# First four feed-forward products as one group in steps of two k-tiles, and most of x turned by VectorE blocks and DRAM instead of TensorE

## The chip, the cores and the metric

The kernel runs on one NeuronCore of a Trainium2 chip. The metric is the device time of one execution in microseconds (us); of several runs the median is taken. The program is launched once; all inputs and the output lie in the chip's DRAM.

## What is computed

One decoder layer on 256 tokens of width 2048, in float32: a half-weighted SwiGLU feed-forward, a mixer (dilated attention beside a gated spatial branch), a second feed-forward and a final norm. The change touches only the first feed-forward's start and the loading of three small parameter rows:

```python
def rmsnorm(x, g):
    r = x32 * lax.rsqrt(jnp.mean(x32 * x32, axis=-1, keepdims=True) + NORM_EPS)
    return (r * g.astype(jnp.float32)).astype(x.dtype)

def swiglu(x, w_gate, w_up, w_down):
    return (jax.nn.silu(x @ w_gate) * (x @ w_up)) @ w_down

# in reference():
x = x + 0.5 * swiglu(rmsnorm(x, ffn1_norm[i]), ffn1_w_gate[i], ffn1_w_up[i], ffn1_w_down[i])
```

`w_gate` and `w_up` are 2048 x 5632, `w_down` is 5632 x 2048.

## The kernel before, in words

**Products.** Every large product is cut into output pieces of 512 columns (`gemm`), each with two PSUM banks, one for each 128 tokens. The sum over the inner dimension goes in k-tiles of 128 rows. A **step** (an entry of `hus`, counted by `i`) is two k-tiles of one piece. Weights come from DRAM in units of four k-tiles (`load_unit`, 1 MB, a `raw` tile, of which there are three); `split` makes of a step's weights a high part (`wh`, ScalarE, L139) and a rest (`wl`, VectorE, L140), of which four pairs exist; the activations are held as such pairs too (`xhi`, `xlo`). `product` (L149) issues one matmul; a step has 12: two k-tiles, two token halves, and the three combinations wh by xhi ("hh"), wl by xhi ("hl") and wh by xlo ("lh"). `high_first` puts the two hl last in each k-tile.

**Order of the work.** The order on each engine is that in which the Python code issues it. The main loop goes over the steps: it issues the products of step `i`, then the callbacks that `at(i, ...)` has left there, then (`advance`) the weight loads that have a free tile and the splits of a later step. `lay_out` writes the list of steps: it goes through the pieces one after the other, the four units of each in turn, and only where `pair` is set are two pieces taken together, with both their last units at the end.

**The transposed x.** A matmul wants the activations with the inner dimension on the partitions. At the start this is done by TensorE: `first_transposes` (L235) turns two 128 x 128 blocks of x for a k-tile, with the identity, into a PSUM bank; `first_evac` multiplies by the norm's weight (`gcols`) and writes `xhi` (ScalarE, L239) and `xlo` (VectorE, L240). All 16 k-tiles of the first norm go this way, 32 transposes, in eight groups of four, placed by `begin` and `ready` between the first steps' matmuls. Everywhere else the kernel uses `turn`: VectorE transposes 32 x 32 blocks (L191), SP writes the result to DRAM (L175), reads it back with the blocks in their places (four reads, L181), and ScalarE and VectorE make the pair of it (L264, L163, L164). The rms itself is applied later, when a product is evacuated, so its squares may be summed after the products have begun.

**The start.** SP issues all loads of weights and x. Seven matmuls on a zeroed tile (`junk`, L81, L748) come ahead of everything on TensorE, then the transpose of the first norm weights (L752), one more such matmul, and then the first transposes of x. x is loaded in parts: columns 0 to 255, 256 to 511, and three times 512. The remaining norm weights are loaded at step 20 and transposed by TensorE at step 60 (`gains`, L761).

Of the kernel before, what the change touches and what calls it, by code (L numbers as in the profile page):

```python
# [8 lines left out]
F32 = mybir.dt.float32  # L9
# [7 lines left out]
P = 128  # L17
# [18 lines left out]
LA = 3  # L36
# [5 lines left out]
def layer(ctx: ExitStack, tc: tile.TileContext, a, out):  # L42
# [25 lines left out]
    rows = sb.tile([60, P], F32, name="rows")  # L68
# [6 lines left out]
    load_rows(0, ACT)  # L75
    half = sb.tile([P, 2], F32, name="half")
# [3 lines left out]
    junk = sb.tile([P, NC], BF16, name="junk")  # L80
    DVE.memset(junk, 0.0)  # L81
# [12 lines left out]
    gcols = sb.tile([P, 60], F32, name="gcols")  # L94
# [6 lines left out]
    def gemm(w, c0, rows0, nk, lhs, post, pair=False):  # L101
        gemms.append(dict(w=w, c0=c0, rows0=rows0, nk=nk, lhs=lhs, post=post, pair=pair))
# [17 lines left out]

    def load_unit(i, parts=(0, 4)):
        g, u, _ = hus[2 * i]
        if i in raws:
            r = raws[i]
        else:
            r = raws[i] = big.tile([P, UK, NC], F32, tag="raw", bufs=RAWB, name=f"raw{i}")
        k0 = g["rows0"] + u * UK * P
        src = g["w"][k0:k0 + UK * P, g["c0"]:g["c0"] + NC].rearrange("(k p) c -> p k c", p=P)
        k = slice(*parts)
        SP.dma_start(r[:, k], src[:, k])  # L130
# [12 lines left out]
    def product(i, jj, t, kind):  # L143
        g, u, j = hus[i]
        if "ps" not in g:
            g["ps"] = [mm_bank(f"mm{i}_{q}") for q in range(NT)]
# [21 lines left out]
    def turn(i, name, q, put, dst, ev, lag=8):  # L168
# [15 lines left out]
        at(i + 3, back)  # L184
# [47 lines left out]
    def first_transposes(k):  # L232
        b = first_banks[k] = first_banks.get(k) or tp_bank(f"xt{k}")
        for t in range(NT):
            PE.transpose(b[:, t * P:(t + 1) * P], x[:, t, k * P:(k + 1) * P], ident)  # L235
# [6 lines left out]
    def residual(e, n, c, banks, scale, norm):  # L242
# [16 lines left out]

        def evac(src):  # L260
            for j in range(4):
# [6 lines left out]
        turn(e + (6 if c == 1 else 2), f"x{n}_{c}", 8, put_tokens(lambda: x[:, :, cs]),  # L268
             lambda: flat(sb.tile([P, NT, NC], F32, tag="gate", bufs=2, name=f"xt{n}_{c}")), evac, 6)


    def ffn(wg, wu, wd, down_post, pair):
        halves = ((0, 6), (6, 11))
        for hf, (f0, f1) in enumerate(halves):
# [8 lines left out]
            for f in range(f0, f1):  # L283
# [30 lines left out]
                gemm(wg, f * NC, 0, KD, lhs_x, post_gate, pair and f == 0)  # L314
                gemm(wu, f * NC, 0, KD, lhs_x, post_up)
            for c in range(4):
                gemm(wd, c * NC, f0 * NC, 4 * (f1 - f0), lhs_h,
                     lambda e, banks, c=c, hf=hf: down_post(e, c, banks, hf == 1), c == 0)
# [5 lines left out]
    ffn(a["ffn1_w_gate"][0], a["ffn1_w_up"][0], a["ffn1_w_down"][0], down1, False)  # L324
# [325 lines left out]
    for j in range(3):  # L650
        gemm(w_in, o_s + j * NC, 0, KD, lhs_x, post_gelu("vs", j), j == 0)
# [12 lines left out]
    for c in range(4):  # L664
        gemm(a["w_out"][0], c * NC, 0, KD, lambda: (mix["mhi"], mix["mlo"]),
             lambda e, banks, c=c: residual(e, 2, c, banks, 1.0, True), c == 0)
# [52 lines left out]
    ffn(a["ffn2_w_gate"][0], a["ffn2_w_up"][0], a["ffn2_w_down"][0], down2, True)  # L719
# [36 lines left out]
    first_banks[1] = mm_bank("xt1")  # L756
    first_banks[2] = mm_bank("xt2")

    def gains():
        b = tp_bank("gc1")  # L760
        PE.transpose(b[:, 0:60], rows, ident[0:60, 0:60])  # L761
        DVE.tensor_copy(gcols[:, 16:60], b[:, 16:60])

    at(20, lambda: [load_rows(i) for i in range(1, 4)])
    at(60, gains)
# [4 lines left out]
    loaded, done = 4, 8  # L770
# [11 lines left out]
    def ready(i, whole=False):  # L782
        ks = (2 * i, 2 * i + 1)
        for k in ks:
            first_transposes(k)
        for j, k in enumerate(ks):
            first_evac(k)
            if not whole:
                split(i, slice(j, j + 1))
        if whole:  # L790
            split(i)

    def begin():
        split(0, slice(0, 1))
        for k in (0, 1):
            first_transposes(k)
            first_evac(k)
        split(0, slice(1, 2))
        products(0, jjs=(0,))
        for t in range(NT):  # L800
            product(0, 1, t, "hh")
        for k in (2, 3):
            first_transposes(k)
            first_evac(k)
        for kind in ("lh", "hl"):
            for t in range(NT):
                product(0, 1, t, kind)
        for k in (0, 1):
            split(1, slice(k, k + 1))

    begin()
    early = {2: (3, False), 3: (4, True), 5: (7, True)}
    midway = {1: (2, False), 3: (5, True), 4: (6, True)}
    for i in range(n):
        if i in early:
            ready(*early[i])
        if 0 < i < n - LA - 1:
# [64 lines left out]
```

## Time and profile before

| | us |
|---|---|
| median of 3 runs (2048.91 to 2049.04) | 2049.03 |
| the profiled execution, its own time | 2049.03 |
| its span (first to last recorded instruction) | 2047.3 |
| TensorE busy in the span | 2037.1 |
| VectorE busy | 1181.6 |
| ScalarE busy | 973.9 |

The span is what the trace covers; 1.7 us of the execution's own time lie around it. PE is TensorE, DVE VectorE, ACT ScalarE, POOL GpSimd; SPq is the queue on which SP issues DMAs. Busy time counts instructions from start to end, and matmuls overlap one another, so a matmul's shown duration is not what it adds to the time; the distance between the starts of two neighbours is.

### The profile page before, as it was taken

What the parts mean: (1) busy time and instruction counts of PE and PEld (TensorE: products, weight loads), DVE (VectorE), ACT (ScalarE), POOL (GpSimd) and SP (SyncE); (2) the same over time, 40 slices, a digit from 0 to 9 for tenths busy, and PEclk for the clock granted to TensorE, in tenths of its full rate; (3) what the DMA queues carried; (4) which work ended last, traced back from release to release, by engine and by line L of the source; (5) the groups of instructions that cost most, each with busy time, mean ns of one, the idle gap of its engine ahead of it and who ended that gap; (6) DMA issues with size and microseconds to landing.
All of it is one profiled execution on the core that took longest, in us unless ns stands there. A gap on an engine that the chain in (4) does not pass through costs nothing.

```text
span 2047.3 us, 23805 instructions
## 1 busy us (share of the span) xinstructions
PE 2037.1 (100%) x9486; PEld 1781.6 (87%) x9486; DVE 1181.6 (58%) x1192; ACT 973.9 (48%) x1070; POOL 12.4 (1%) x18
## 2 busy tenths in 40 slices
PE   9999999999999999999999999999999999999998
PEld 7888888888888888888888888888888888888887
DVE  5555555555556557665665555565555555555554
ACT  6444444444445555455554444564444444444443
POOL 0000000000000000000000000000000000000000
PEclk9999999999999999999999999999999999999999
DMA  7777876666776866787866666777777666777764
GB/s 271 234 236 226 272 245 216 201 222 224 243 229 220 269 201 201 238 280 257 262 212 224 225 225 207 245 250 235 220 243 226 226 205 205 221 222 242 232 214 144
DMA packets 246775, 469.35 MB, mean 229 GB/s; under 512 B 11084, under 2 KB 38536, under 8 KB 246536
## 3 DMA queue, kind: packets, MB, share of 16 engines
q1 hardware_dynamic: 246344, 467.30, 70.4%
q8 instruction: 74, 1.21, 0.2%
q10 hardware_dynamic: 320, 0.53, 0.1%
q14 instruction: 37, 0.30, 0.0%
HBM read 439.22 MB, written 28.57 MB: 228 GB/s over the span
## 4 chain that ended last, share of the span: by engine, by line
PE 99%; issue 0%; ACT 0%; DVE 0%; POOLq 0%; POOL 0%
PE mm L149 98%; PE sc L560 0%; PE sp L458 0%; PE warm L748 0%; PE pv L600 0%; PE sc L562 0%; PE xt L235 0%; PE pv L596 0%; ACT x L716 0%; ACT xhi L239 0%; PE pv L597 0%; DVE x L701 0%; POOLq L877 0%; POOL rf L708 0%; ACT wh L139 0%
## 5 line engine op out<-in xcount | busy, mean ns | idle before, releaser
L140 DVE TENSOR_TENSOR wl<-raw,wh 128x1024 fp32r<-128x1024 f32 (+1 forms) x780 | 948.1, 1218 | 822.1 <-ACT wh L139 818.0
L139 ACT ACTIVATE wh<-raw 128x1024 fp32r<-128x1024 f32 (+1 forms) x780 | 818.0, 1052 | 1007.6 <-PE mm L149 974.6
L149 PE MATMUL mm<-wh,xhi 128*128 128x512 f32 x2144 | 813.8, 380 | 0.5 <-ACT wh L139 0.4
L149 PE MATMUL mm<-wh,xlo 128*128 128x512 f32 x2144 | 812.5, 379 | 0.0
L149 PE MATMUL mm<-wl,xhi 128*128 128x512 f32 x2144 | 811.8, 379 | 0.0
L149 PEld LDWEIGHTS mm<-wh,xhi 128*128 128x128 f32 x2144 | 405.3, 189 | 58.5 <-ACT wh L139 0.8
L149 PEld LDWEIGHTS mm<-wl,xhi 128*128 128x128 f32 x2144 | 405.4, 189 | 57.2
L149 PEld LDWEIGHTS mm<-wh,xlo 128*128 128x128 f32 x2144 | 405.1, 189 | 57.3
L149 PE MATMUL mm<-wh,hhi 128*128 128x512 f32 x704 | 266.8, 379 | 0.0
L149 PE MATMUL mm<-wl,hhi 128*128 128x512 f32 x704 | 266.8, 379 | 0.0
L149 PE MATMUL mm<-wh,hlo 128*128 128x512 f32 x704 | 266.8, 379 | 0.0
L149 PEld LDWEIGHTS mm<-wh,hhi 128*128 128x128 f32 x704 | 133.1, 189 | 18.9
L149 PEld LDWEIGHTS mm<-wl,hhi 128*128 128x128 f32 x704 | 133.1, 189 | 18.9
L149 PEld LDWEIGHTS mm<-wh,hlo 128*128 128x128 f32 x704 | 133.1, 189 | 18.9
L149 PE MATMUL mm<-wh,uT 128*128 128x512 f32 x192 | 58.0, 379 | 0.0
L149 PE MATMUL mm<-wh,mhi 128*128 128x512 f32 x128 | 48.5, 379 | 0.0
L149 PE MATMUL mm<-wl,mhi 128*128 128x512 f32 x128 | 48.5, 379 | 0.0
L149 PE MATMUL mm<-wh,mlo 128*128 128x512 f32 x128 | 48.5, 379 | 0.0
L149 PEld LDWEIGHTS mm<-wh,uT 128*128 128x128 f32 x192 | 36.3, 189 | 5.1
L149 PE MATMUL mm<-wl,uT 128*128 128x512 f32 x96 | 36.4, 379 | 0.0
L304 DVE SCALAR_TENSOR_TENSOR sg<-mm,rstd,sg 128x512 f32<-128x512 f32 x44 | 30.9, 744 | 0.0
L219 ACT ACTIVATE junk<-x 128x512 bf16<-128x512 f32 x30 | 18.9, 629 | 25.0 <-DVE x L247 18.6
(142 smaller groups left out, 596.9 us busy)
## 6 DMA issues: line engine op xcount, KB each, us to landing
raw<-in_w_in_dram SPq DMA_DIRECT2D x92, 1024.0 KB, 5.1
raw<-in_ffn_w_up_dram SPq DMA_DIRECT2D x88, 1024.0 KB, 5.2
raw<-in_ffn_w_down_dram SPq DMA_DIRECT2D x88, 1024.0 KB, 5.1
raw<-in_ffn_w_gate_dram SPq DMA_DIRECT2D x84, 1024.0 KB, 5.1
raw<-in_w_out_dram SPq DMA_DIRECT2D x16, 1024.0 KB, 5.0
raw<-in_w_sg_out_dram SPq DMA_DIRECT2D x12, 1024.0 KB, 5.8
bmh<-bth SPq DMA_DIRECT2D x22, 512.0 KB, 2.9
sg<-bmh SPq DMA_DIRECT2D x88, 128.0 KB, 5.0
```

Of the source, the lines that this page charges most:

```text
L139: ACT.activation(wh[:, k], r[:, k], AF.Copy)
L140: DVE.tensor_tensor(wl[:, k], r[:, k], wh[:, k].bitcast(F32), op=OP.subtract)
L149: PE.matmul(g["ps"][t], act[:, k, t * P:(t + 1) * P], in_turn(w[:, jj]), start=k == 0 and kind == "hh", stop=k == g["nk"] - 1 and kind == ...
L219: ACT.activation(junk, x[:, t, c * NC:(c + 1) * NC], AF.Square, accum_out=ss[n][:, t, c:c + 1])
L304: DVE.scalar_tensor_tensor(two(sg[:, t]), banks[t], rstd[:, t:t + 1], two(sg[:, t]), op0=OP.mult, op1=OP.mult)
```

## The change

1. `lay_out` sorts steps, not units. The first four pieces of the first feed-forward (gate 0, up 0, gate 1, up 1) form one group (`FIRST`): first k-tiles 0 and 1 of all four (steps 0 to 3), then k-tiles 2 and 3 of all four (steps 4 to 7), then k-tiles 4 to 7 of each piece (steps 8 to 15), then k-tiles 8 to 15 of each (steps 16 to 31). The other groups (`PAIR`) give the same order as before. The third and fourth piece accumulate in the banks that the transposes use (tag `tp`).
2. `load_unit` can fill a `raw` tile from two weights; the first four units are loaded so.
3. Only k-tiles 0 to 3 of the first x are transposed by TensorE. Columns 512 to 2047 go through `turn_x`, as the later norms do: columns 512 to 1023 at step 0 (read back at 1, made into pairs at 4), the next 512 at steps 7, 10 and 12, the last at 8, 11 and 13. The loads of the last 1024 columns of x are issued after steps 3 and 4.
4. The remaining norm weights are loaded at step 32 and go through a VectorE block transpose, a DRAM write and four small reads; TensorE's `gains` is gone.
5. `junk` is zeroed before `half` and `pad`.

```diff
-    def gemm(w, c0, rows0, nk, lhs, post, pair=False):
+    def gemm(w, c0, rows0, nk, lhs, post, group=(1, ()), bank=None):
...
-            gs = gemms[i:i + 2] if gemms[i]["pair"] else gemms[i:i + 1]
-            i += len(gs)
-            units = [(g, u) for g in gs for u in range(g["nk"] // UK)]
-            if len(gs) == 2:
-                units.sort(key=lambda q: q[1] == q[0]["nk"] // UK - 1)
-            for g, u in units:
-                hus.extend([(g, u, 0), (g, u, 1)])
+            size, bounds = gemms[i]["group"]
+            steps = [(g, q) for g in gemms[i:i + size] for q in range(g["nk"] // 2)]
+            i += size
+            steps.sort(key=lambda s: sum(s[1] >= (b if b > 0 else s[0]["nk"] // 2 + b) for b in bounds))
+            hus.extend((g, q // 2, q % 2) for g, q in steps)
+
+    PAIR = (2, (-2,))
+    FIRST = (4, (1, 2, 4))
...
+    def turn_x(i, n, c, lag, read=3):
         def evac(src):
...
+        turn(i, f"x{n}_{c}", 8, put_tokens(lambda: x[:, :, c * NC:(c + 1) * NC]),
+             lambda: flat(sb.tile([P, NT, NC], F32, tag="gate", bufs=2, name=f"xt{n}_{c}")), evac, lag, read)
...
+                bank = tp_bank if group is FIRST and f == 1 else mm_bank
...
     load_unit(0, (0, 1))
     load_x(0, S)
-    load_unit(0, (1, 2))
+    for i, k in ((0, 1), (0, 2), (0, 3), (1, 0), (1, 1)):
+        load_unit(i, (k, k + 1))
+    load_x(NC, 2 * NC)
+    for k in (2, 3):
+        load_unit(1, (k, k + 1))
     load_x(S, NC)
-    load_unit(0, (2, 3))
-    load_unit(0, (3, 4))
-    for c in range(1, 4):
-        load_x(c * NC, (c + 1) * NC)
-        load_unit(c, (0, 2))
-        load_unit(c, (2, 4))
+    load_unit(2)
...
-    at(20, lambda: [load_rows(i) for i in range(1, 4)])
-    at(60, gains)
+    for i, fn in ((32, more_rows), (36, rows_out), (40, rows_back)):
+        at(i, fn)
...
-    begin()
-    early = {2: (3, False), 3: (4, True), 5: (7, True)}
-    midway = {1: (2, False), 3: (5, True), 4: (6, True)}
+    for c, i, lag, read in ((1, 0, 4, 1), (2, 7, 5, 3), (3, 8, 5, 3)):
+        turn_x(i, 0, c, lag, read)
+    for c in (2, 3):
+        at(c + 1, lambda c=c: load_x(c * NC, (c + 1) * NC))
...
+    split(0, slice(0, 1))
+    first_x((0, 1))
+    for i, k in ((0, 1), (1, 0), (1, 1), (2, 0), (2, 1)):
+        split(i, slice(k, k + 1))
     for i in range(n):
...
+        if i < n - LA - 1:
+            products(i, jjs=(0,), high_first=i < 4)
+            if i == 2:
+                first_x((2, 3))
+            products(i, jjs=(1,), high_first=i < 4)
```

Where it moves instructions, first on TensorE. This is the stretch around the second and third group of four transposes before; `wh1` and `wl1` are the weights of step 1, `xt4` to `xt7` banks of transposed x.

```order
L149 MATMUL mm0_0_138<-wl1_162,xhi0_118 128x512
L149 MATMUL mm0_1_139<-wl1_162,xhi0_118 128x512
L235 MATMUL xt4_173<-ident_76,x_81 128x128 x2
L235 MATMUL xt5_176<-ident_76,x_81 128x128 x2
L149 MATMUL mm0_0_138<-wh1_161,xhi0_118 128x512
L149 MATMUL mm0_0_138<-wh1_161,xlo0_119 128x512
L149 MATMUL mm0_1_139<-wh1_161,xhi0_118 128x512
L149 MATMUL mm0_1_139<-wh1_161,xlo0_119 128x512
L149 MATMUL mm0_0_138<-wl1_162,xhi0_118 128x512
L149 MATMUL mm0_1_139<-wl1_162,xhi0_118 128x512
L235 MATMUL xt6_195<-ident_76,x_81 128x128 x2
L235 MATMUL xt7_198<-ident_76,x_81 128x128 x2
```

And this is the one place after the first products at which the changed kernel transposes x on TensorE, in the middle of step 2, and the start of step 3 (`mm3`).

```order
L155 MATMUL mm2_0_191<-wl2_141,xhi0_115 128x512
L155 MATMUL mm2_1_192<-wl2_141,xhi0_115 128x512
L241 MATMUL xt2_199<-ident_76,x_81 128x128 x2
L241 MATMUL xt3_202<-ident_76,x_81 128x128 x2
L155 MATMUL mm2_0_191<-wh2_140,xhi0_115 128x512
L155 MATMUL mm2_0_191<-wh2_140,xlo0_116 128x512
L155 MATMUL mm2_1_192<-wh2_140,xhi0_115 128x512
L155 MATMUL mm2_1_192<-wh2_140,xlo0_116 128x512
L155 MATMUL mm2_0_191<-wl2_141,xhi0_115 128x512
L155 MATMUL mm2_1_192<-wl2_141,xhi0_115 128x512
L155 MATMUL mm3_0_231<-wh3_168,xhi0_115 128x512
```

Six of the eight groups are gone, and the banks `xt2` and `xt3` are those that `mm3` accumulates in: step 3 waits until VectorE has emptied them.

On VectorE the changed kernel has, around steps 2 to 4, the block transposes of x's columns 512 to 1023 (`btx0_1`) between the splits, and the rests of k-tiles 2 and 3 (`xt2`, `xt3`) behind the split of step 3:

```order
L146 TENSOR_TENSOR wl2_141<-raw1_93,wh2_140 128x512 x2
L197 STREAM_TRANSPOSE btx0_1_160<-x_81 128x4x4x32 x2
L146 TENSOR_TENSOR wl3_169<-raw1_93,wh3_168 128x1024
L246 SCALAR_TENSOR_TENSOR xlo0_116<-xt2_199,gcols_84,xhi0_115 128x256
L246 SCALAR_TENSOR_TENSOR xlo0_116<-xt3_202,gcols_84,xhi0_115 128x256
L146 TENSOR_TENSOR wl4_218<-raw2_100,wh4_217 128x1024
```

Before, the rests of k-tiles 2 and 3 stood ahead of the split of step 1, and no block transpose was there.

SP's queue before, from the first instruction:

```order
L130 DMA raw0_87<-in_ffn1_w_gate_dram 128x512
L88 DMA x_81<-in_x_dram 128x2x256
L130 DMA raw0_87<-in_ffn1_w_gate_dram 128x512
L88 DMA x_81<-in_x_dram 128x2x256
L130 DMA raw0_87<-in_ffn1_w_gate_dram 128x512 x2
L88 DMA x_81<-in_x_dram 128x2x512
L130 DMA raw1_95<-in_ffn1_w_gate_dram 128x2x512 x2
L88 DMA x_81<-in_x_dram 128x2x512
L130 DMA raw2_99<-in_ffn1_w_gate_dram 128x2x512 x2
L88 DMA x_81<-in_x_dram 128x2x512
```

and in the changed kernel, after the same three rows (`bmx0_1` is the write of the turned blocks to DRAM, `xt0_1` what is read back):

```order
L135 DMA raw0_87<-in_ffn1_w_up_dram 128x512 x2
L135 DMA raw1_93<-in_ffn1_w_gate_dram 128x512 x2
L88 DMA x_81<-in_x_dram 128x2x512
L135 DMA raw1_93<-in_ffn1_w_up_dram 128x512 x2
L88 DMA x_81<-in_x_dram 128x2x256
L135 DMA raw2_100<-in_ffn1_w_gate_dram 128x2x512
L135 DMA raw2_100<-in_ffn1_w_up_dram 128x2x512
L181 DMA bmx0_1_163<-btx0_1_160 128x1024
L135 DMA raw3_165<-in_ffn1_w_gate_dram 128x2x512
L135 DMA raw3_165<-in_ffn1_w_up_dram 128x2x512
L187 DMA xt0_1_186<-bmx0_1_163 32x4x256 x4
L135 DMA raw4_215<-in_ffn1_w_gate_dram 128x4x512
```

The columns 256 to 511 of x now come eleventh instead of fourth, and the write and the reads of the turned part stand ahead of the weights of steps 6 to 9.

## Rows read from the trace of the kernel before

**Rows 1.** Busy time by engine in two stretches of the span: stretch in us and its length, then for each engine busy us and (x instructions), the granted clock of TensorE as a share of full speed, the DMA engines' mean busy share, and GB/s moved.

```profile
0.00:10.00 10.00, 8.27 (x29) 4.78 (x29) 3.56 (x10) 4.85 (x10) 0.70 (x6) 1.00 0.75 243
...
400.00:2000.00 1600.00, 1600.00 (x7462) 1401.91 (x7461) 935.04 (x936) 767.02 (x835) 2.99 (x3) 1.00 0.71 230
```

**Rows 2.** The chain of work that ended last, in order of time, its first pieces: start in us, length in us, engine, tile, line and number of instructions.

```profile
5.24 0.44 PE xt L235 x2
5.71 0.48 ACT xhi L239
6.23 2.19 PE mm L149 x8
...
8.68 0.84 ACT xhi L239 x2
9.52 0.53 ACT wh L139
10.09 1.56 PE mm L149 x6
11.65 0.44 PE xt L235 x4
...
22.91 0.44 PE xt L235 x4
23.35 145.04 PE mm L149 x672
```

**Rows 3.** Groups of instructions, different shapes apart: line, engine, operation, tiles, shapes and count, then busy us in all and mean ns of one, then idle time before them and what ended it.

```profile
L139 ACT ACTIVATE wh<-raw 128x1024 fp32r<-128x1024 f32 x772 | 813.0, 1056 | 1006.6 <-PE mm L149 974.6 <-DMA raw<-in_w_in_dram 14.6 <-DVE rp L507 7.7
L140 DVE TENSOR_TENSOR wl<-raw,wh 128x1024 fp32r<-128x1024 f32 x772 | 942.7, 1224 | 822.0 <-ACT wh L139 818.0
L240 DVE SCALAR_TENSOR_TENSOR xlo<-xt,gcols,xhi 128x256 fp32r<-128x256 f32 x16 | 7.2, 480 | 4.0 <-ACT xhi L239 4.0
L239 ACT ACTIVATE xhi<-xt,gcols 128x256 fp32r<-128x256 f32 x16 | 7.0, 471 | 6.6 <-PE xt L235 6.6
L235 PE MATMUL xt<-ident,x 128*128 128x128 f32 x32 | 5.3, 291 | 0.0
L139 ACT ACTIVATE wh<-raw 128x512 fp32r<-128x512 f32 x8 | 4.9, 628 | 1.0 <-DMA raw<-in_ffn_w_gate_dram 1.0
L140 DVE TENSOR_TENSOR wl<-raw,wh 128x512 fp32r<-128x512 f32 x8 | 5.4, 687 | 0.1
```

**Rows 4.** TensorE's matmuls in order of time around the transpose of the remaining norm weights: start, duration, engine, line, operation, tiles, shape, count.

```profile
168.01 0.38 PE L149 MATMUL mm<-wh,xlo 128*128 128x512 f32 x1
168.32 0.27 PE L761 MATMUL gc<-ident,rows 60*128 60x60 f32 x1
168.52 0.48 PE L149 MATMUL mm<-wh,xhi 128*128 128x512 f32 x1
168.84 0.38 PE L149 MATMUL mm<-wl,xhi 128*128 128x512 f32 x1
```

**Rows 5.** VectorE's instructions before the first transposes, in order of time, columns as in rows 4.

```profile
0.88 0.06 DVE L77 MEMSET half<- 128x2 f32 x1 [0.88 <-PEq L865]
0.91 0.06 DVE L79 MEMSET pad<- 128x2 f32 x1
0.99 0.27 DVE L81 MEMSET junk<- 128x256 uint32 x1
```

**Rows 6.** SP's DMA issues in order of time: start of the issue, its duration, line, tiles, count (a row with x2 stands for two).

```profile
1.26 0.42 SPq L88 DMA_DIRECT2D x<-in_x_dram  x1
1.73 0.46 SPq L130 DMA_DIRECT2D raw<-in_ffn_w_gate_dram  x1
2.23 0.61 SPq L88 DMA_DIRECT2D x<-in_x_dram  x1
...
3.87 0.43 SPq L88 DMA_DIRECT2D x<-in_x_dram  x1
4.35 1.70 SPq L130 DMA_DIRECT2D raw<-in_ffn_w_gate_dram  x2
6.10 0.90 SPq L88 DMA_DIRECT2D x<-in_x_dram  x1
```

**Rows 7.** The same issues with their size and the us from issue to landing, in the same order: those of 1.26, 1.73, 2.23, 3.87, the first of the two of 4.35, and that of 6.10.

```profile
x<-in_x_dram SPq DMA_DIRECT2D x1, 256.0 KB, 3.5
raw<-in_ffn_w_gate_dram SPq DMA_DIRECT2D x1, 256.0 KB, 4.7
x<-in_x_dram SPq DMA_DIRECT2D x1, 256.0 KB, 5.6
x<-in_x_dram SPq DMA_DIRECT2D x1, 512.0 KB, 6.5
raw<-in_ffn_w_gate_dram SPq DMA_DIRECT2D x1, 512.0 KB, 7.3
x<-in_x_dram SPq DMA_DIRECT2D x1, 512.0 KB, 8.2
```

**Rows 8.** A later norm's turn through DRAM, that of x's first 512 columns behind the first feed-forward: VectorE's block transposes, SP's write and four reads, and the making of the pair, each from its engine's instructions in order of time.

```profile
644.17 1.30 DVE L191 STREAM_TRANSPOSE btx<-x 128x512 f32<-128x512 f32 x2
...
645.49 0.34 SPq L175 DMA_DIRECT2D bmx<-btx  x1
...
648.39 1.75 SPq L181 DMA_DIRECT2D xt<-bmx  x4
...
656.71 1.69 ACT L264 ACTIVATE xt<-xt,gcols 128x256 f32<-128x256 f32 x4
658.43 1.06 ACT L163 ACTIVATE xhi<-xt 128x1024 fp32r<-128x1024 f32 x1
...
659.52 1.23 DVE L164 TENSOR_TENSOR xlo<-xt,xhi 128x1024 fp32r<-128x1024 f32 x1 [1.46 <-ACT xhi L163]
```

**Rows 9.** Time from issue to landing over all eight such turns, shortest, median and longest: first of the write to DRAM, then of the reads.

```profile
DMA to landing us min/median/max: 2.7/2.8/3.6
...
DMA to landing us min/median/max: 4.2/4.9/6.1
```

More of the change, by code (lines that the diff above doesn't have):

```diff
@@ L65, in two @@
         return ap.rearrange("p (a c) -> p a c", a=2)
-    rows = sb.tile([60, P], F32, name="rows")
+    rows = sb.tile([64, P], F32, name="rows")
     def load_rows(i, queue=SP):
@@ L75, in layer @@
     load_rows(0, ACT)
+    junk = sb.tile([P, NC], BF16, name="junk")
+    DVE.memset(junk, 0.0)
     half = sb.tile([P, 2], F32, name="half")
@@ L99, in layer @@
     callbacks = {}
-    def gemm(w, c0, rows0, nk, lhs, post, pair=False):
-        gemms.append(dict(w=w, c0=c0, rows0=rows0, nk=nk, lhs=lhs, post=post, pair=pair))
+    def gemm(w, c0, rows0, nk, lhs, post, group=(1, ()), bank=None):
+        gemms.append(dict(w=w, c0=c0, rows0=rows0, nk=nk, lhs=lhs, post=post, group=group, bank=bank or mm_bank))
     def lay_out():
@@ L121, in load_unit @@
     def load_unit(i, parts=(0, 4)):
[L122 to L130, printed above, removed]
+        if i not in raws:
+            raws[i] = big.tile([P, UK, NC], F32, tag="raw", bufs=RAWB, name=f"raw{i}")
+        (g, u, j), (h, v, _) = hus[2 * i], hus[2 * i + 1]
+        first, last = parts
+        while first < last:
+            end = last if (g, u) == (h, v) or first > 1 else min(last, 2)
+            q, w, k = (g, u, 0) if first < 2 else (h, v, 2)
+            o = 2 * hus[2 * i + k // 2][2] - k if (g, u) != (h, v) else 0
+            k0 = q["rows0"] + w * UK * P
+            src = q["w"][k0:k0 + UK * P, q["c0"]:q["c0"] + NC].rearrange("(k p) c -> p k c", p=P)
+            SP.dma_start(raws[i][:, first:end], src[:, first + o:end + o])
+            first = end
     def split(i, k=slice(0, 2)):
@@ L145, in product @@
         if "ps" not in g:
-            g["ps"] = [mm_bank(f"mm{i}_{q}") for q in range(NT)]
+            g["ps"] = [g["bank"](f"mm{i}_{q}") for q in range(NT)]
         k = u * UK + 2 * j + jj
@@ L164, in split_psum, with turn @@
         DVE.tensor_tensor(lo, src, hi.bitcast(F32), op=OP.subtract)
-    def turn(i, name, q, put, dst, ev, lag=8):
+    def turn(i, name, q, put, dst, ev, lag=8, read=3):
         got = {}
@@ L183, in turn @@
         at(i, blocks)
-        at(i + 3, back)
+        at(i + read, back)
         at(i + lag, lambda: ev(got["e"].rearrange("p (i m b) -> p m i b", i=4, b=32)))
@@ L266, in evac, with ffn @@
             split_psum(turned(xT["hi"][:, ks]), turned(xT["lo"][:, ks]), src)
[L268 to L272 removed]
+        turn(i, f"x{n}_{c}", 8, put_tokens(lambda: x[:, :, c * NC:(c + 1) * NC]),
+             lambda: flat(sb.tile([P, NT, NC], F32, tag="gate", bufs=2, name=f"xt{n}_{c}")), evac, lag, read)
+    def ffn(wg, wu, wd, down_post, group):
         halves = ((0, 6), (6, 11))
@@ L755, in layer, with more_rows, rows_out, rows_back @@
     norm_open(0)
[L756 to L762, printed above, removed]
-    at(20, lambda: [load_rows(i) for i in range(1, 4)])
-    at(60, gains)
+    def more_rows():
+        POOL.memset(rows[32:64], 0.0)
+        for i in range(1, 4):
+            load_rows(i)
+    def rows_out():
+        d = sb.tile([64, P], F32, name="gd")
+        DVE.transpose(d.rearrange("p (j b) -> p j b", b=32), rows.rearrange("p (j b) -> p j b", b=32))
+        xT["gains"] = m = dram.tile([64, P], F32, name="gm")
+        SP.dma_start(m, d)
+    def rows_back():
+        m = xT["gains"].rearrange("(i a) (j b) -> j a i b", a=32, b=32)
+        for j in range(4):
+            SP.dma_start(gcols[32 * j:32 * j + 32].rearrange("p (i b) -> p i b", i=2), m[j])
+    for i, fn in ((32, more_rows), (36, rows_out), (40, rows_back)):
+        at(i, fn)
     for c in range(4):
@@ L768, in layer @@
     at(12, lambda: norm_rstd(0))
-    loaded, done = 4, 8
+    loaded, done = 3, 3
     def advance(to):
```

60 lines of the change are left out of this document (14 added, 46 removed).

## The prediction

> **What bounds the kernel now.** I read first where TensorE stands still. From 400 to 2000 us it is busy in the whole of 1600 us, at full granted clock; in the first 10 us it is busy for 8.27 [rows 1]. So every instruction taken off TensorE after the start is worth the distance it makes between its neighbours, and work on other engines costs nothing until something on TensorE waits for it. Then the chain of waits, from its beginning: it enters the first product at 6.23 us through two transposes of x and ScalarE's `xhi`, leaves TensorE once more (8.68 to 10.09, `xhi` and `wh` on ScalarE), and from 10.09 on is TensorE alone: matmuls, and groups of four transposes [rows 2]. A matmul is worth 145.04 / 672 = 0.216 us, a group of four transposes 0.44 us [rows 2]. What the change can do lies in the first 23 us and at 168 us; behind that the lists of steps are the same.
>
> The profiled execution took 2049.03 us, which is also the median, so the sum is made against 2049.03.
>
> **The first 23 us.** Up to 23.35 us TensorE has done 60 products (five steps: 23.35 is where the sixth begins) and, after 6.23, seven groups of transposes. Products start with 0.46 us more than eight times 0.216 (2.19 less 1.73) [rows 2]. If the changed kernel starts its products at the same 6.23 and nothing holds it, it has the same 60 products after 0.46 + 60 x 0.216 = 13.41 us, and one group, 0.44: at 20.08. The gain is 23.35 - 20.08 = **3.27 us**. Six groups are 2.64 of it (6 x 0.44); the other 0.63 is the trip through ScalarE of 8.68 to 10.09, which came because the second k-tile's transposes stood in the middle of step 0, and `xhi` of k-tiles 2 and 3 ahead of step 1's `wh`. Now four pieces need only k-tiles 0 and 1 for four steps, 48 products or 10.4 us, and these two are ready together at the start.
>
> The transposes are a place where rows read otherwise than they look. One is shown with 291 ns on average [rows 3], but four stand in 0.44 us of the chain, 0.11 each; they overlap. The Trainium skill ("TensorE: Matmul & The Clock Gate", "Part 4: PE-mode transpose") gives about 275 ns for one in a kernel's context; as a duration the row agrees, and by it 24 transposes would be an estimated 6.6 us instead of 2.64.
>
> **At 168 us.** The transpose of the norm weights lies between two products: from the lh before it to the second product after it 168.84 - 168.01 = 0.83 us pass, where two distances of 0.216 would be [rows 4]: 0.40 us gained. The block transpose that replaces it is one instruction on VectorE at step 36 with nothing near waiting for it, and its DMAs (three loads that were there before, one write, four reads) are small; VectorE has 665 us of 1600 free [rows 1]. The weights are first used by the next norm. I cost it at nothing.
>
> **`junk` first.** The chain begins with VectorE's memsets; `half` and `pad` start at 0.88 and 0.91, `junk` at 0.99 [rows 5]. Moved ahead, it is up to 0.11 us earlier, and the warming matmuls with it. What may keep the gain away is the first x, landed at 1.26 + 3.5 = 4.76 [rows 6, 7], about 0.5 us before the transposes in the chain. Between 0 and 0.11 I take 0.10, as 4.76 is still early enough.
>
> **What could be late: step 3.** Its two banks are those of k-tiles 2 and 3, so it waits for VectorE's two `xlo`, which stand behind two block transposes and the split of step 3. Landings come in order of issue. Before, 0.75 MB of the first loads had landed at 1.73 + 4.7 = 6.43, 1.0 at 2.23 + 5.6 = 7.83, 2.0 at 10.37, 2.5 at 11.65 and 3.5 at 14.3 [rows 6, 7]. I take the same curve for the new order. The second k-tile of step 0 is the third load as before; step 1's two weights (1.0 and 1.25 MB) land by 8.5, before TensorE needs them at 9.0 and 10.3. x's columns 512 to 1023 (2.25 MB) land at 11.0, the weights of step 3 (2.75 MB) at 12.3, columns 256 to 511 (3.0 MB) at 13.0. TensorE, at 6.13 + 0.46 + 30 x 0.216, wants those at 13.1, so the transposes just pass. ScalarE's `wh` of step 3 then ends at 13.4, VectorE's rest (1.22) at 14.6, and two `xlo` (0.48 each) at 15.55 [rows 3]. Step 3 would begin at 14.65 without that; its first product can go at 15.1 and its third, in the second bank, at 15.6, where 15.1 was due: **0.45 us lost**. Bounds: nothing, if the landings of the new order come 0.5 us earlier than on the curve; 1.2 us if step 3's weights land 0.75 us later (under a third of the 2.6 us between 5.6 and 8.2 [rows 7]).
>
> **Step 8, the first that needs a turned k-tile.** It starts at 28.2 (96 products and a group behind 6.13, plus 0.45). The turn: x landed 11.0, behind two splits VectorE turns it until 12.4 (1.30 for the pair [rows 8]). The write is queued behind 4 MB of loads: 2.8 us alone [rows 9], but not before the curve's 15.5 plus 1.3, so 16.8. Four reads take 1.75 to issue [rows 8], 16.8 to 18.5, and land 4.9 later, counted from the start of the last issue at 18.2: 23.1 [rows 9]. ScalarE and VectorE need 1.69 + 1.06 + 1.23 for the pair [rows 8], and VectorE 1.22 more for step 8's rest [rows 3]: 28.3 at the latest, where the second product of step 8 at 28.4 wants it. Nothing lost, by a hair: with reads of 6.1 us it is 1.1, with 4.2 there is 0.8 to spare. Behind the reads in SP's queue wait the weights of steps 8 to 11, wanted from 28.2 on; issued at 18.7 and 19.2 they have eight us. The third and fourth turn have eight and ten more steps; I find the pair for step 16 ready about 1 us early, so the same lateness would show there again, but not twice, as each wait pushes the later need too.
>
> ScalarE in steps 8 to 19 has twelve splits of 1.06, eight sums of squares and two pairs of 2.75, some 25 us in 31: no bound.
>
> **Sum.** 2049.03 - 3.27 - 0.40 - 0.10 + 0.45 = **2045.7 us**, 0.16% less. A measurement of this kernel can tell about 0.2% from no change, 4.1 us, so this counts as within.
>
> **Rivals.**
> - *The turn comes late by a little.* For it: no margin at step 8, a read's landing spread of 1.9 us [rows 9], a full queue. Against: the median read just fits. 1.2 us more: 2046.9.
> - *Slower.* Three DMA trips in a row (x in, blocks out, blocks back) at the longest landing of the loaded start, 8.2 us [rows 7]: x at 4.1 + 8.2 = 12.3, turned 13.6, out 21.8, reads issued until 23.3 and landed at 31.5, pair and rest 5.2 more: 36.7 against 28.4, a wait of 8.3 us at step 8, less 3.77 gained: 2053.6. It decides when the reads land later than 27. For it: DMA queues are full at the start. Against: later turns never needed more than 3.6 and 6.1 [rows 9]. The Trainium skill ("VectorE: DVE Perf Modes", "Rules for kernel authors") says to turn 128 x 128 on TensorE if PSUM will do as the destination, which speaks for the kernel before; these rows put 0.11 us of the bounding engine against time on free ones.
> - *Transposes cost what they show.* 24 x 0.291 = 6.98 instead of 2.64 [rows 3]: 2041.4. Against it stands the chain's 0.44 for four [rows 2].
> - *The start is bound by loads anyway.* If weights of steps 1 to 3 land as late as the gain, all 3.27 us turn into waits on `wh`: 2048.5. Against: before, x's 2 MB stood among the first loads, now 1 MB of it comes later.
>
> **How the numbers follow.** The forecast (no wait, or one at step 3 only) has 0.62, the turn late by a little 0.25, the load-bound start 0.05, slower 0.04, the dear transposes 0.02; 0.02 stays for a start that gains half a microsecond more than I see, which passes 4.1. So faster 0.04, same 0.92, slower 0.04. Range: at the low end no wait anywhere and the whole 0.11, 2045.25, with 0.25 for the execution to execution spread and my rounding: 2045.0; at the high end 1.2 at step 3 and 1.7 at steps 8 and 16: 2048.2.
>
> **What would show it.** Right: the chain starts its products at about 6.1, has one group of transposes at about 13, no trip to ScalarE near 9, a wait of `mm` on VectorE's `xlo` of at most 1.2 us near 15, and is TensorE alone from there, also through 28 and 49 us; the distance at 168 us is gone. Wrong: a wait near 28 or 49 on the turned pair (the turn is late), waits on `wh` before 15 (loads), or products that start later than 6.2.

## The result: 2056.2 us, slower by 0.33%, and the profile after

The changed kernel takes 2056.19 us in the median of six runs (2053.53 to 2056.6), the kernel before 2048.94 (2048.47 to 2049.04) beside it: a ratio of 1.0033 [1.0023, 1.0044]. 2045.7 was forecast, in a range of 2045.0 to 2048.2. The forecast is wrong, in sign too. The profiled execution took 2056.16 us, its span is 2054.4, so the sum is made against 2056.16.

**Where TensorE waits.** These are the matmuls and transposes of the first 63 us that had to wait, and the first few at a slower clock, in order of time (start, duration, then in brackets the idle time before it and what ended it):

```profile
5.56 0.48 PE L155 MATMUL mm<-wh,xhi 128*128 128x512 f32 x1 [0.35 <-ACT xhi L245]
13.43 0.63 PE L241 MATMUL xt<-ident,x 128*128 128x128 f32 x4 [0.82 <-DMA x<-in_x_dram]
15.45 0.48 PE L155 MATMUL mm<-wh,xhi 128*128 128x512 f32 x1
...
49.25 0.38 PE L155 MATMUL mm<-wh,xlo 128*128 128x512 f32 x1
50.93 0.48 PE L155 MATMUL mm<-wh,xhi 128*128 128x512 f32 x1 [1.30 <-ACT wh L145]
52.38 0.48 PE L155 MATMUL mm<-wl,xhi 128*128 128x512 f32 x1 [0.96 <-DVE wl L146]
...
54.64 0.38 PE L155 MATMUL mm<-wh,xlo 128*128 128x512 f32 x1
57.52 0.48 PE L155 MATMUL mm<-wh,xhi 128*128 128x512 f32 x1 [2.50 <-ACT wh L145]
58.96 0.79 PE L155 MATMUL mm<-wl,xhi 128*128 128x512 f32 x1 [0.96 <-DVE wl L146]
59.55 0.63 PE L155 MATMUL mm<-wh,xlo 128*128 128x512 f32 x1
...
62.03 0.38 PE L155 MATMUL mm<-wh,xlo 128*128 128x512 f32 x1
```

50.93 is the first product of step 16, 57.52 the first of step 17. By the distance of 0.216 us from the product before it, the four starts are late by 1.46 (49.47 was due), 1.24, 2.66 and 1.22 us. From 58.96 to 62.03 seven distances take 3.07 instead of 1.51: 1.56 more. Together **8.14 us**, in 13 us of the program, and at the place that the forecast had named as its sign of being wrong ("a wait near 28 or 49 on the turned pair"), though by way of `wh`. The granted clock in that stretch (columns of the windows as in [rows 1], the number before the last two is the clock):

```profile
56.00:58.00 2.00, 0.48 (x1) 0.19 (x1) 1.45 (x2) 2.00 (x3) 0.00 (x0) 1.00 0.00 0
...
59.00:60.00 1.00, 1.00 (x3) 0.82 (x4) 1.00 (x2) 1.00 (x2) 0.00 (x0) 0.50 0.01 2
60.00:61.00 1.00, 1.00 (x4) 0.81 (x3) 1.00 (x2) 0.31 (x1) 0.00 (x0) 0.50 0.86 162
...
62.00:63.00 1.00, 1.00 (x6) 0.86 (x6) 0.31 (x1) 0.00 (x0) 0.00 (x0) 1.00 1.04 403
```

After having stood still for most of 54.9 to 59.0, TensorE runs at half its clock (0.50, the level of 1.2 GHz) until some 3 us later.

**The chain of waits** of this stretch, which before was TensorE alone from 10.09 on [rows 2]:

```profile
19.47 9.44 DMA raw<-in_ffn_w_up_dram
29.02 1.07 ACT wh L145
...
32.58 6.36 DMA bmx<-btx
38.95 6.19 DMA xt<-bmx
45.15 8.47 DMA xt<-bmx
53.73 1.71 ACT xt L273 x4
55.46 1.06 ACT xhi L169
56.55 0.98 DVE xlo L170
57.69 1.23 DVE wl L146
58.96 770.73 PE mm L155 x3563
```

It goes through the turns: VectorE's blocks, the second turn's write to DRAM (6.4 us, the third's took 5.3; [rows 9] had 2.7 to 3.6), the reads back, and the making of the pair on ScalarE. The reads' time from issue to landing, first of the second turn (issued at 38.95 to 40.7), then of the third (41.2 to 45.5), stands against 4.2 to 6.1 in [rows 9]:

```profile
DMA to landing us min/median/max: 6.2/6.5/6.8
...
DMA to landing us min/median/max: 8.5/9.6/10.8
```

**Why step 17 waits for the third turn**, of which it uses nothing (it multiplies by k-tiles 10 and 11 of the first piece, which are the second turn's; the third turn's are first needed in step 18), is to be seen on ScalarE, in order of time:

```profile
47.13 1.71 ACT L273 ACTIVATE xt<-xt,gcols 128x256 f32<-128x256 f32 x4 [4.96 <-DMA xt<-bmx]
48.87 1.06 ACT L169 ACTIVATE xhi<-xt 128x1024 fp32r<-128x1024 f32 x1
49.84 1.04 ACT L145 ACTIVATE wh<-raw 128x1024 fp32r<-128x1024 f32 x1
53.73 1.71 ACT L273 ACTIVATE xt<-xt,gcols 128x256 f32<-128x256 f32 x4 [2.85 <-DMA xt<-bmx]
55.46 1.06 ACT L169 ACTIVATE xhi<-xt 128x1024 fp32r<-128x1024 f32 x1
56.42 3.88 ACT L145 ACTIVATE wh<-raw 128x1024 fp32r<-128x1024 f32 x4
```

The `wh` at 49.84 is step 16's; it stands behind the second turn's pair. The first of the four at 56.42 is step 17's; it stands behind the third turn's pair, which waits for reads that land at 53.6. The weights were there by then: once the pair is done, four splits follow without a pause.

**Step 16 to 17 is not all.** Near 880 us, in the mixer, one more wait stands in this profile. Around it the rest of the program falls 1.4 us further behind (the first product on `sp` is 5.63 us behind before's at 824, that on `sc` 7.05 at 989; the wait shown is 0.85 of it by the distance of the starts):

```profile
881.46 0.48 PE L155 MATMUL mm<-wl,xhi 128*128 128x512 f32 x1 [0.69 <-DVE wl L146]
```

### The profile page after: what moved, and what is told of

It reads as the page before. It is cut to its first block, busy times and chain, and to the rows that moved or that the text cites. A ratio compares the mean times of both kernels' runs of the same rounds, so it can differ in the third digit from the quotient of the medians.

```text
span 2054.4 us, 23799 instructions
## 1 busy us (share of the span) xinstructions
PE 2036.9 (99%) x9461; PEld 1779.0 (87%) x9461; DVE 1182.8 (58%) x1188; ACT 977.5 (48%) x1072; POOL 13.4 (1%) x19
## 4 chain that ended last, share of the span: by engine, by line
PE 95%; DMA 3%; DVE 1%; issue 0%; ACT 0%; SPq 0%; POOLq 0%; POOL 0%; ACTq 0%; DVEq 0%
PE mm L155 94%; DMA raw<-in_w_in_dram 1%; DMA xt<-bmx 1%; DMA bmx<-btx 1%; DMA raw<-in_ffn_w_up_dram 0%; DMA x<-in_x_dram 0%; DVE wl L146 0%; PE sc L570 0%; PE sp L468 0%; PE pv L610 0%; PE sc L572 0%; ACT wh L145 0%; SPq L135 0%; SPq L187 0%; DVE btx L197 0%
```

## The experiments

Two theories follow from this profile. **Order:** step 17's weights stand in line behind a pair that only step 18 needs. **Load:** the turns' three trips meet a DMA queue that is backlogged by the weights and by x's second half, so that each trip takes twice its usual time. The kernel before ran beside every run: medians of 2049.0 to 2049.03 us, 97 runs in all, between 2048.39 and 2050.89.

**1. The third turn's pair two steps later.**

```diff
-    for c, i, lag, read in ((1, 0, 4, 1), (2, 7, 5, 3), (3, 8, 5, 3)):
+    for c, i, lag, read in ((1, 0, 4, 1), (2, 7, 5, 3), (3, 8, 7, 3)):
```

> The changed kernel with one number changed: the third turn's pair (x columns 1536 to 2047) is made at step 15 instead of 13. Its k-tiles are first needed at step 18. Order theory (step 17's weight split only waits because it stands on ScalarE behind a pair whose reads land at 53.6): the waits of 2.50 and 0.96 us at step 17 go, and with them the stretch at half clock (about 1.3 us); 2056.2 - 4.7 = 2051.5. Load theory (the DMA queues carry too much in the first 55 us and the weights of steps 18 and 19 are late as well): the wait moves to step 18 and stays over 2 us, 2054 or more.

2051.2 us (2047.8 to 2053.45; 1.0009 [1.0, 1.0018]), 5 us less than the changed kernel. TensorE's waits between 14 and 800 us:

```profile
50.80 0.48 PE L155 MATMUL mm<-wh,xhi 128*128 128x512 f32 x1 [0.76 <-ACT wh L145]
52.25 0.48 PE L155 MATMUL mm<-wl,xhi 128*128 128x512 f32 x1 [0.96 <-DVE wl L146]
```

None at step 17. The clock falls behind step 16's instead, to 0.50 from 53 to 56 us, where it had stayed at 1.00 in the changed kernel's profile. So the order is worth 5 of the 7.25 us by which the changed kernel is slower than the kernel before; step 16 is still late.

**2. The group of products without the turns.** The first two products as the group, all of x turned by TensorE in the middles of seven steps. The loads of x are moved forward for it: columns 256 to 511 are sixth in the queue instead of eleventh.

```diff
-    FIRST = (4, (1, 2, 4))
+    FIRST = (2, (1, 2, 4))
...
+    middle = {1: (2, 3), 2: (4, 5), 3: (6, 7), 5: (8, 9), 6: (10, 11), 7: (12, 13), 8: (14, 15)}
...
-            if i == 2:
-                first_x((2, 3))
+            if i in middle:
+                first_x(middle[i])
```

> The grouping alone: the first two pieces as a group in the same steps of two k-tiles, all 16 k-tiles of x turned by TensorE as before, none through DRAM; the norm weights' turn and the early zeroing of junk as in the change. Both theories: no wait near 49 us, since neither the turned reads nor their load is there. All eight groups of transposes stay, so of the forecast gain 0.63 (start) + 0.40 (168 us) + 0.1 to 0.7 (start of the first product) is left: 2047.3, between 2047.1 and 2048.0. If the grouping itself were what costs, over 2050.

2050.39 us (2049.84 to 2051.63; 1.0008 [0.9999, 1.0017]): a miss. No wait at 49 us, but the start is bound by loads, as its chain shows (start, length):

```profile
5.12 6.36 DMA raw<-in_ffn_w_up_dram
11.56 1.06 ACT wh L145
12.65 1.22 DVE wl L146
13.87 0.41 DVE xlo L246
14.32 1.35 PE mm L155 x5
```

The load issued at 5.12 is the eighth of weights, for step 3. Its split stands on VectorE ahead of the `xlo` that step 3's transposed k-tiles need, so TensorE waits for the load though the products at hand have their weights. So this run doesn't price the turns alone. It shows that loads can bind the start, which is the forecast's fourth rival, but in another order of loads than the changed kernel's.

**3. Four levels of k, the turns spread out.** The second turn begins at step 5 instead of 7, its x is loaded one weight unit earlier, the third is not needed before step 24 and goes at steps 14 to 20; the squares, and what waits for them, are six steps later.

```diff
-    FIRST = (4, (1, 2, 4))
+    FIRST = (4, (1, 2, 4, 6))
...
+                if loaded == 5:
+                    load_x(2 * NC, 3 * NC)
...
-    for c, i, lag, read in ((1, 0, 4, 1), (2, 7, 5, 3), (3, 8, 5, 3)):
+    for c, i, lag, read in ((1, 0, 4, 1), (2, 5, 7, 3), (3, 14, 6, 3)):
```

> The changed kernel with a fourth level in the group: k-tiles 8 to 11 of all four pieces in steps 16 to 23, 12 to 15 in steps 24 to 31; the second turn two steps earlier (its x loaded between the weights of steps 8 and 10) with its pair at 12 as before, the third at steps 14, 17 and 20, its x loaded at step 8; sums of squares from step 14. Order theory: nothing stands behind a pair that has not landed, waits near 49 and 57 us go: 2056.2 - 7.0 = 2049.2, and 2047.8 if the 1.4 us lost near 880 us go as well. Load theory: the third turn's 1.5 MB leave the first 50 us too, so the same; if the reads of the second turn are late by themselves, a wait of 1 to 2 us stays at step 16: 2050 to 2051.

2047.24 us (2045.79 to 2047.8; 0.999 [0.9981, 0.9999]), the fastest of the kernels that leave nothing out, and 0.6 us better than the better of the two times expected. Its chain is TensorE alone from 15 us to the mixer:

```profile
14.98 805.76 PE mm L155 x3732
```

Its runs lie around 2046.0 and 2047.6, and the profiled one (2046.02) has no wait in the mixer: with the turns in time, the start gives in this execution what the forecast's terms said. What the executions near 2047.6 lost was not seen.

**4. The small parts alone:** the kernel before with the norm weights by VectorE and DRAM, and `junk` first (items 4 and 5 of the change).

```diff
-        b = tp_bank("gc1")
-        PE.transpose(b[:, 0:60], rows, ident[0:60, 0:60])
-        DVE.tensor_copy(gcols[:, 16:60], b[:, 16:60])
...
+        DVE.transpose(d.rearrange("p (j b) -> p j b", b=32), rows.rearrange("p (j b) -> p j b", b=32))
```

> The kernel before with only two parts of the change: the later norm weights through VectorE and DRAM instead of TensorE at step 60, and junk zeroed first. By the forecast 0.40 + 0.10 less: 2048.4. If the early zeroing is also what let the changed kernel begin its products 0.67 us earlier, 2047.9. If the norm weights' DMAs cost something that the forecast left out, no less than 2048.9.

2048.47 us (2048.05 to 2049.86; 0.9998 [0.999, 1.0007]), 0.5 less than before. The interval alone would not tell that from nothing, but the profile does: the products start at 6.17 instead of 6.23, and the first product on `sp` comes 0.57 earlier. The terms of 0.40 and 0.10 stand about as forecast.

**5 to 7. Again, and with the DRAM tiles exchanged.** The changed kernel unaltered; the changed kernel and the kernel before with one unused tile set aside, so that every turn uses the other of the two DRAM tiles.

```diff
     lay_out()
     n = len(hus)
+    dram.tile([P, 4, 256], F32, tag="turn", name="skip")
```

> The changed kernel itself, unaltered, beside the next ones. Order theory (step 17's weights stand on ScalarE behind the third turn's pair) and load theory (the second turn comes out of a backlog of loads) both say 2056 us again, with waits of 1.3 and 2.5 us on wh at steps 16 and 17, since nothing in them is chance. What is open is the wait of 1.4 us in the mixer near 880 us: if it belongs to the kernel it stands there again; if it is a matter of DMA packets' chance order it is smaller or gone in some executions, and the times scatter between 2054.7 and 2056.2.

> One unused DRAM tile is set aside ahead of the first turn, so every later turn writes to the other of its two DRAM tiles; nothing else differs. If the three extra turns of the changed kernel cost the mixer 1.4 us by changing which DRAM tile its turns use, the wait near 880 us goes and the time is 2054.7. If the place in DRAM has nothing to do with it, 2056.2 and the wait of 0.7 us on wl near 881 us is there. The waits at steps 16 and 17 stay the same by every theory.

> The kernel before with the same unused DRAM tile. If the choice of DRAM tile is what costs the mixer 1.4 us, this one gets the wait near 875 us: 2050.4. If not, 2049.0.

2055.59 us (2050.99 to 2059.15; 1.003 [1.0019, 1.004]), 2055.28 (2050.96 to 2057.02; 1.0029 [1.0018, 1.0041]) and 2048.93 (2048.56 to 2049.32; 1.0 [0.9991, 1.0009]). None of the three profiles has a wait in the mixer, that of the unaltered kernel included, so it comes and goes by itself. In the kernel before, the other DRAM tile alone does not bring it: all ten runs stay below 2049.4. That the waits at 16 and 17 would repeat was wrong as well: they differ from profile to profile, and the times of the unaltered kernel scatter over 8 us. But the order holds in each. In the second execution of the unaltered kernel, on ScalarE and then on TensorE:

```profile
52.09 1.70 ACT L273 ACTIVATE xt<-xt,gcols 128x256 f32<-128x256 f32 x4 [2.46 <-DMA xt<-bmx]
```

```profile
51.14 0.48 PE L155 MATMUL mm<-wl,xhi 128*128 128x512 f32 x1 [0.35 <-DVE wl L146]
55.88 0.48 PE L155 MATMUL mm<-wh,xhi 128*128 128x512 f32 x1 [2.10 <-ACT wh L145]
```

From the start of the third pair to step 17's first product it is 55.88 - 52.09 = 3.79 us here, 57.52 - 53.73 = 3.79 in the first profile, 57.02 - 53.22 = 3.80 in that with the tiles exchanged. Step 16 waits for nearly nothing here, and step 17 still waits: it follows the third turn, not step 16.

**8. The second turn two steps earlier, the third's pair two later.**

```diff
+                if loaded == 5:
+                    load_x(2 * NC, 3 * NC)
...
-    for c, i, lag, read in ((1, 0, 4, 1), (2, 7, 5, 3), (3, 8, 5, 3)):
+    for c, i, lag, read in ((1, 0, 4, 1), (2, 5, 7, 3), (3, 8, 7, 3)):
...
-    for c in (2, 3):
-        at(c + 1, lambda c=c: load_x(c * NC, (c + 1) * NC))
+    at(4, lambda: load_x(3 * NC, D))
```

> The changed kernel with three edits: x's third quarter is loaded ahead of the sixth weight unit instead of behind it, its turn is begun at step 5 instead of 7 (pair still at step 12), and the third turn's pair is made at step 15 instead of 13. Load theory: x's third quarter lands near 28.5 instead of 30.1, the blocks are written at 29 instead of 32.6, the reads are issued near 34.5 instead of 39 and land by 43; then no wait on wh at step 16 (before 0.76 us with the pair at 15 alone), none at step 17, TensorE alone from 15 us on, and 2047.3 us, or 2048.7 with the mixer's wait. If the second turn is late because reads in 1 KB pieces are slow whatever stands before them, the wait at step 16 stays over 0.5 us and the time is 2051.

2047.45 us (2046.83 to 2049.42; 0.9994 [0.9984, 1.0003]). The second turn's reads were issued at 34.26 and landed 3.6 us later; no wait at 16 and 17. The third's pair could begin at 51.5 only, and step 18 waited 0.8 for its pair in the profiled run (2049.42, the longest, with the mixer's wait in it).

**9. Without the third turn.** It is left out, and k-tiles 12 to 15 get a pair made from the second turn's tile.

```diff
-    for c, i, lag, read in ((1, 0, 4, 1), (2, 7, 5, 3), (3, 8, 5, 3)):
+    for c, i, lag, read in ((1, 0, 4, 1), (2, 7, 5, 3)):
...
+            if n == 0 and c == 2:
+                ks = slice(12, 16)
+                at(13, lambda: split_psum(turned(xT["hi"][:, ks]), turned(xT["lo"][:, ks]), src))
```

> The changed kernel without the third turn: its block transposes, its write, its four reads and its four scalings are left out, and k-tiles 12 to 15 get the pair made from the second turn's tile (so that part of the product is of other numbers; the time of the products is the same). The last quarter of x is still loaded. Order theory: the wait at step 17 is there because that step's wh stands on ScalarE behind the third turn's pair, which waits for its reads; without them no wait at step 17 over 0.5 us and no half clock behind it, 5.4 us less (2.66 + 1.22 + 1.56 in the changed kernel's profile). If the third turn's transfers also held up the second's, the wait at step 16 shrinks too, down to 2047.3; if the backlog is the weights' and x's alone, the second turn's reads still land near 47, the waits at step 16 stay at up to 2.3, and the time is 2050. If the loss were the queue's alone and had nothing to do with ScalarE's order, step 17 would still wait.

2047.75 us (2046.46 to 2049.43; 0.9994 [0.9984, 1.0003]). No wait at step 16 or 17. The second turn's reads were issued at 39.12, as in the changed kernel, but landed like this:

```profile
DMA to landing us min/median/max: 3.7/3.9/4.1
```

against 6.2 to 6.8 above. So a good part of the second turn's lateness is the third turn's: its write stands in the queue ahead of the second's reads, and its own reads right behind them. The second turn's write was no faster: it was issued at 31.84, and the reads, which wait for it, not before 39.12. That part of the lateness is not the third turn's. Load theory, as I had it (weights and x alone), says too little.

**10. A quarter of the weights** in units 4 to 9.

```diff
-                load_unit(loaded)
+                load_unit(loaded, (0, 1) if 4 <= loaded <= 9 else (0, UK))
...
+        if 4 <= i // 2 <= 9:
+            r = raws[i // 2][:, 0:1, :].to_broadcast([P, 2, NC])
```

> The changed kernel with a quarter of the load in weight units 4 to 9 (steps 8 to 19): one k-tile of four is loaded, and the splits read it twice, so these steps compute with other weights at the same cost. 4.5 MB of 6 are left out between 18 and 41 us. Load theory (the turns are late because their trips stand in a backlog of weights and x): the loads of x's second half land in about 5 us instead of 10, the blocks' writes in about 3 instead of 6, the reads in about 5 instead of 6 to 10, as the later turns' do; no wait at steps 16 and 17, and 2047.3, or 2048.7 with the mixer's wait. Rival: reads in 1 KB pieces land as late by themselves, with two turns behind each other; then the reads still take over 6, step 17 still waits, and the time is above 2051.

2047.11 us (2046.01 to 2049.47; 0.9991 [0.9981, 1.0]). The issues between 30 and 46 us, with their size and the median from issue to landing, first of the changed kernel, then here:

```profile
raw<-in_ffn_w_gate_dram SPq DMA_DIRECT2D x2, 1024.0 KB, 9.7
bmx<-btx SPq DMA_DIRECT2D x2, 512.0 KB, 5.8
xt<-bmx SPq DMA_DIRECT2D x8, 128.0 KB, 8.5
```

```profile
bmx<-btx SPq DMA_DIRECT2D x2, 512.0 KB, 2.8
xt<-bmx SPq DMA_DIRECT2D x8, 128.0 KB, 4.7
```

Both trips fall to about half, to the times of [rows 9], with two turns behind each other as before. Reads in 1 KB pieces are not late by themselves, the backlog makes them so; and no wait is left at 16 and 17 though their order is unchanged.

**11. Three turns added to the kernel before,** at steps 60 to 62, with results that nothing uses.

```diff
+    for c in (1, 2, 3):
+        cs = slice(c * NC, (c + 1) * NC)
+        turn(59 + c, f"d{c}", 8, put_tokens(lambda cs=cs: x[:, :, cs]),
+             lambda c=c: flat(sb.tile([P, NT, NC], F32, tag="gate", bufs=2, name=f"dd{c}")), lambda src: None, 6)
```

> The kernel before with three turns of x added at steps 60, 61 and 62, whose results nothing uses: VectorE's block transposes, the writes and the reads. In the profiles of the changed kernel the mixer's wait of up to 1.4 us near 880 us comes and goes, and in those of the kernel before it is not seen. If three more turns anywhere ahead shift how the mixer's transfers meet (the count of DMAs issued, the DRAM tiles), the times scatter by 1.5 us here as well, up to 2050.5. If they have nothing to do with it, 2049.0 with little scatter.

2050.5 us (2049.91 to 2050.82; 1.0007 [0.9998, 1.0016]), but not by the mixer, which has no wait. The chain of waits near step 69 (start, length; `dd` is what an added turn reads back, `bth` the blocks of the next turn of the kernel itself):

```profile
183.15 5.44 DMA dd<-bmd
188.72 1.30 DVE bth L191 x2
190.03 1.12 DVE wl L140
191.19 634.60 PE mm L149 x2939
```

The blocks of the next turn take the tile that an added turn's reads are still landing in, and a split stands behind them on VectorE: TensorE stops for 1.79 us, though no product needs the added turns. It is a loss of the same kind as the changed kernel's, on VectorE instead of ScalarE. More turns ahead of it do not bring the mixer's wait.

**12. The third turn behind the second's reads.**

```diff
-    for c, i, lag, read in ((1, 0, 4, 1), (2, 7, 5, 3), (3, 8, 5, 3)):
+    for c, i, lag, read in ((1, 0, 4, 1), (2, 7, 5, 3), (3, 11, 6, 3)):
```

> The changed kernel with one number of it changed: the third turn starts at step 11 instead of 8 (read at 14, pair at 17), so its write stands in SP's queue behind the second turn's reads instead of ahead of them, and its pair on ScalarE behind the weights of step 17. Nothing is left out. If the second turn's reads are late because the third's write is ahead of them and its reads right behind them, they land as in the run without a third turn, about 5.5 us after their issue near 39, so by 45; no wait at step 16 over 0.3, none at step 17, and the third's pair is ready for step 18 at 54: 2047.3 us, up to 2048.7 with the mixer's wait in it. If the backlog of weights and x alone makes them late, steps 16 waits as with the pair at 15 (0.76 and 0.96): 2049 to 2051.

2052.22 us (2049.75 to 2055.18; 1.0017 [1.0008, 1.0027]). The half of it that was to be told apart came as expected: the second turn's pair began at 42.25, and steps 16 and 17 did not wait. The other half missed: the third turn itself is late, at step 18, and the clock falls again behind it (0.50 from 58 to 60). TensorE's first product of step 18, and ScalarE's pair before it:

```profile
56.77 0.48 PE L155 MATMUL mm<-wh,xhi 128*128 128x512 f32 x1 [2.69 <-ACT xhi L169]
```

```profile
53.92 1.70 ACT L273 ACTIVATE xt<-xt,gcols 128x256 f32<-128x256 f32 x4 [1.34 <-DMA xt<-bmx]
```

From its blocks at 39.53 to the pair at 53.92 it took 14.4 us. With three levels of k both turns are wanted within two steps, and one of them is late; later need (run 3) or less traffic (9, 10) takes that away, an earlier begin (8) all but 0.8 us of it.

## Why the prediction was wrong

**The step that failed** is the second half of "Step 8": "I find the pair for step 16 ready about 1 us early, so the same lateness would show there again, but not twice". Three things in it:

- *The size.* Only the first turn was worked out: its write by the curve of the loaded queue (12.4 to 16.8, so 4.4 us), its reads by [rows 9] (4.9 us). They took 4.5 (12.66 to 17.12) and 4.1 to 4.6 us, and the pair was begun at 23.21, where the reads were to land at 23.1. Step 8 did not wait for it; only its second product came 0.13 us late, behind a `wl` whose `wh` had waited 0.47 us for weights. For the second and third turn "about 1 us early" stands without a sum, as if their trips took no longer. They took 5.3 to 6.4 and 6.2 to 10.8 us, because their writes and reads share the queue with the weights and with one another. Runs 9 and 10 show both parts: without the third turn the second's reads take 3.9, with a quarter of the weights both turns take 2.8 and 4.7 us. (What x's last 1 MB adds was not taken out by itself.) I had not asked when the load of the queue ends. TensorE came to step 16 2.2 us ahead of the kernel before (due at 49.47, against 51.68), and each turn adds 1 MB of traffic, so the queue had less time for more bytes.
- *The order.* "Not twice, as each wait pushes the later need too" holds for what needs the pair, step 18 on. Step 17 doesn't need the third pair, but its `wh` is issued behind it. The second wait comes by ScalarE's order, not by need, and is the larger: 2.66 + 1.22 against 1.46 + 1.24. Run 1 takes it away by that alone; in run 12, which takes it away too, the write has moved as well. I had counted ScalarE's busy time ("25 us in 31: no bound") and not who stands behind an instruction that waits.
- *The clock.* 1.56 us more for starting again at half clock, which the forecast has nowhere.

The rival on the other side (2053.6, with 0.04) had the load half of the mechanism, three trips in a row in a loaded queue; it looked for it at step 8, where 27 us decided and 23.1 was forecast. Its chance was far too small, because it was weighed at the one place and not at steps 16 and 17.

**What held.** Step 3's wait: 0.45 forecast; its first product came 0.26 after it was due. (By the forecast's own terms step 3 was due at 6.13 + 0.46 + 36 x 0.216 + 0.44 = 14.81 and not at 14.65, so the sum should have had about 0.3.) Step 8: nothing lost to the turn. The distance at 168 us, and `junk`: run 4. The price of the transposes: the one group left takes 0.38 us from 13.43 to 13.81, 0.10 each where 0.11 was taken. The gain of the start, in run 3: 2046.02 in its profiled execution, against 2045.7, though the median is 2047.24.

**What was off and small.** Products start at 5.56, not 6.1, in this execution (6.17 in the profiles of runs 5 and 6), which is luck. The transposes of k-tiles 2 and 3 waited 0.82 for x, which took 7.0 us from its issue at 6.26, where "just pass" was forecast. At the end of step 15 TensorE was at 49.47, 48.92 by the forecast's terms: 0.55 late. 2045.7 + 0.55 + 8.14 + 1.42 is 2055.8, 0.35 less than measured.

The Trainium skill's rule ("VectorE: DVE Perf Modes", "Rules for kernel authors"), to turn 128 x 128 on TensorE if PSUM will do, comes out right for this change as it stands. In run 3, with the turns spread out, it does not: 2047.24 against 2049.0, an interval of the ratio that ends at 0.9999. The price was not the turn's instructions but when its trips land.

**Open** is the mixer's wait of up to 1.4 us: seen in the profiles of the changed kernel, of runs 1, 8 and 9, not in those of 2 to 7 and 10 to 12 nor before. The reads into `q` there begin 38.1 us after the first product on `sp`, 36.9 before; but in runs 3 and 6, which have no such wait, it is 38.7 and 38.4, so this does not decide it. In the kernel before, neither the other DRAM tile (7) nor three more turns (11) brings the wait; what of the new start reaches so far was not found.

## What to carry to other kernels

A transfer's duration from a quiet stretch is no price for it in a backlogged one: before moving work from a bounding engine to DMA, add up the bytes due in that stretch and ask when the backlog ends, above all if the change itself makes the engine earlier. And for every instruction that may wait, read on its engine what is queued behind it: work that doesn't need the late data is late all the same. Where two DRAM turns are wanted in the same steps, give one of them later need rather than a later start.

## What the runs showed of the hardware

*The turns' reads fill the DMA engines without filling the rate.* While they run, in pieces of 1 KB, the engines' busy share is as high as under weight loads in pieces of 2 KB, but the rate is much lower. The size of the pieces by itself is not the reason: x's columns 256 to 511 come in pieces of 1 KB too, and in the microsecond from 11 to 12, when 165 of the 276 pieces moved were theirs, the rate was nearly that of the weights. (Changed kernel, windows: the x load among weights, weights alone, and the reads among weights; the last two columns are DMA share and GB/s.)

```profile
11.00:12.00 1.00, 1.00 (x6) 0.88 (x5) 0.68 (x2) 0.00 (x0) 0.00 (x0) 1.00 1.07 396
...
24.00:30.00 6.00, 6.00 (x28) 4.98 (x27) 3.59 (x3) 4.96 (x8) 0.00 (x0) 1.00 1.05 409
...
42.00:48.00 6.00, 6.00 (x30) 5.25 (x29) 1.47 (x3) 1.04 (x4) 0.91 (x2) 1.00 1.04 243
```

The Trainium skill ("DMA: Bandwidth & Descriptors", "Specifications") gives 512 B as the least transfer for line rate; the x load agrees with that (396 GB/s with pieces of 1 KB), and the turns' reads, of the same piece, stay at 243. One of these reads goes to 32 partitions, the load of x to 128, and the reads take from DRAM what was written there just before; which of these differences makes them slow, or whether it is another, no run here separates.

*The clock falls after a short stop in a busy program.* With 2.50 and 0.96 us idle in a row (or 2.10 and 0.96 in run 5, or 2.69 and 0.56 in run 12) TensorE was granted 0.50 of its clock for about 3 us afterwards; but also behind the 0.76 and 0.96 of run 1, while behind the changed kernel's 1.30 and 0.96, at step 16, and behind the 1.79 of run 11 it stayed at 1.00. So the length of one stop does not tell it; such a fall cost 1.56 us for seven matmuls here.
